# Half of the S5 chunk matrices made in the prologue, a third adaLN part made in the projections, products in stored order

## The chip, the cores and the metric

One core of one Trainium2 chip runs one inference step through two trunk layers. The metric is the device time of the whole program in microseconds (us).

## The reference, cut to what matters

```python
def trunk_layer(x, cmod, P, l, cache):
    sh1, sc1, g1, sh2, sc2, g2 = adaln(cmod, P['w_mod'][l], P['b_mod'][l])   # silu(c) @ w_mod + b, six parts
    h = rmsnorm(x, P['g_norm1'][l]) * (1.0 + sc1) + sh1
    z, xbc, dt_raw, u, dq, dk, dv, wq, wk, wv = split(h @ P['w_in'][l])
    # four mixers: SSD (z, xbc, dt), S5 (u), differential attention (dq, dk, dv), windowed attention (wq, wk, wv)
    merged = sum_i sigmoid(h @ w_gate + b_gate)_i * (y_i @ w_branch_i) @ P['w_out'][l]
    x = x + g1 * merged                                       # g1 is the third adaLN part
    h2 = rmsnorm(x, P['g_norm2'][l]) * (1.0 + sc2) + sh2
    return x + g2 * (square(relu(h2 @ P['w_fc1'][l])) @ P['w_fc2'][l])

def s5_direction(u, lam, log_step, b, c, s0):                 # per group of 16 channels, 64 complex states
    ab = exp(lam * exp(log_step)); coef = (ab - 1) / lam
    s[t] = ab * s[t-1] + coef * (b @ u[t]);  y[t] = real(c @ s[t])
```

There are 1024 channels, 640 tokens (128 of context, 512 latent), and everything is float32.

## The kernel before, in words

Activations lie with channels on partitions and 640 tokens along the free axis, in two halves of 320. A dense product is made from two-part operands: `load_w` loads a weight tile of 128x512, ACT rounds it to the high part `wh` (L211), and DVE or, for every third tile, POOL subtracts to get the low part `wl` (L195); each product is then three matmuls (L222 to L224). Weight loads are given priority ahead of the rest.

The order of the instructions on each engine is fixed when the program is built: a planner walks a simulated time line and issues what is ready, the earlier in the text first, so every engine runs a fixed queue in order. Within the "mix" stage the text itself is ordered by letter strings (`PLAN`, L58 to L72): each letter advances one generator (L1637 to L1660) by one step. In the string `pre`, which runs first, `b` is a step of `s5_build`, `u` of the S5 input projection, `v` of the keys and values of the windowed attention, `g` a gate panel, `d` a step of `adgen`, the adaLN parts made ahead.

The program starts with a prologue (L1550 to L1608). Its loop over q = 0..4 makes the adaLN parts 0 and 1 (shift and scale) in four panels (`panel_adaln`, L1562, and `adaln`, L278: matmuls of L287, a copy by ACT at L292, matmuls with `sel` at L294, the sum on DVE at L297), from 512 KB loads into a ring of 14 tiles `wm`; loads x; takes the norm (L352 to L371) and makes the normed activations `h` in high and low parts as panels come (`norm_mod`, L376 to L403, on DVE, ACT and POOL); and multiplies the first two tiles of the S5 input projection (L1593). After the loop it makes adaLN part 2 in four more panels (L1599).

`s5_build` (L473 to L672) turns the S5 parameters into chunk matrices. Its first step is a setup of some hundred operations on 128x32 tiles, mostly on DVE (L484 to L582). Then come eight builds, one for every four groups: `bt` and `bz` (L606 to L615); the input-side product `pt` (L625 to L628), made by `cmul`, which multiplies once on DVE into `s5u` (L592), once on POOL into `s5v` (L593) and combines on DVE (L594), twice for 128x512 elements; its transposes through PSUM (L633) and a copy (L636) to DRAM; the output-side product `qt` in the same way (L640 to L644); and the kernel matrix `pk` (L646 to L671). A build writes three times 512 KB to DRAM. Setup and builds are held back until the last element of `h` is made: POOL copies that element into a tile that they write next (L486, L608). One setup and eight builds thus run behind the prologue, the builds all in `pre`. Layer 1 has its own setup and eight builds inside the MLP of layer 0.

`pt` is stored in the order (group, channel m, position s) but computed in the order (group, s, m): its inner index m steps by 8 elements in the result (L626).

Of the kernel before, what the change touches and what calls it, by code (L numbers as in the profile page):

```python
# [13 lines left out]
F32 = mybir.dt.float32  # L14
# [4 lines left out]
ALU = mybir.AluOpType  # L19
# [34 lines left out]
SCAN = 5  # L54

LOW = 3
WM = 14
PLAN = dict(  # L58
    ad_out=((2, 2, 2, 1, 1), (0, 0, 0, 0, 0)),
    pre=("bbbuuvbubvbvbgvgggbvgvv", ""),  # L60
    mix=(
        "sisppppppiiippsisisasgssssappsssaxssgpsappxgxaaiagaaaagxcgaoogoccxcclooxscggcglgllccglPgogcgAPPA"
        "zPAAzcAAzwPzzzmmzPzPoozwPPwwwPwwAPwwmAmAmmnmmAPnnmnPnnninnfcqqcffwqkkqqfffkkkqkkkfkqkfwqhwwfhkfh"
# [12 lines left out]
def hybrid_body(ctx: ExitStack, tc: tile.TileContext, a: dict, o: dict, dbg: dict):  # L76
# [47 lines left out]
    def pb1():  # L124
        return pp.tile([128, 512], F32, tag="pb", name=nm("pb"), bufs=1)
# [11 lines left out]
    def ring(tag, cols, where="pool"):  # L137
        def get(shape, name, dt=F32):
            n = int(np.prod(shape[1:]))
            t = top[where].tile([128, cols], dt, tag=tag, name=nm(name), bufs=RINGS[tag])[:, :n]  # L140
            if len(shape) == 2:
                return t
            letters = "abcdef"[: len(shape) - 1]
            dims = dict(zip(letters, shape[1:]))
            return t.rearrange(f"p ({' '.join(letters)}) -> p {' '.join(letters)}", **dims)

        return get
# [3 lines left out]
    t1, tx, tq = ring("t1", 320), ring("tx", 652), ring("tq", 256)  # L151
    ty, tw, td = ring("ty", 1024, "right"), ring("tw", 648, "right"), ring("td", 640, "right")

    nt, wa = ring("nt", 320), ring("wa", 512)

    def big(shape, tag, dt=F32, bufs=1, where="pool"):

        return top[where].tile(list(shape), dt, tag=tag, name=nm(tag), bufs=bufs)
# [311 lines left out]

    s5m = {}

    def s5_build(l, where, after):  # L473

# [121 lines left out]
        for b in range(8):  # L598
            g0 = 4 * b
            late = after()  # L600
            braw = big([128, 2, 4, 16], "s5b", bufs=2, where=where)
            sp.dma_start(out=braw, in_=a["s5_b"][l, b])
            craw = big([128, 2, 4, 16], "s5c", bufs=2, where=where)
            sp.dma_start(out=craw, in_=a["s5_c"][l, b])

            bt = big([128, 2, 4, 16], "s5bt", where=where)  # L606
            if late is not None:
                nc.gpsimd.tensor_copy(out=bt[0:1, 0, 0, 0:1], in_=late)  # L608
            cmul(bt[:, 0], bc(cre, g0, 16), braw[:, 0], bc(cim, g0, 16), braw[:, 1], ALU.subtract, [128, 4, 16])
            cmul(bt[:, 1], bc(cre, g0, 16), braw[:, 1], bc(cim, g0, 16), braw[:, 0], ALU.add, [128, 4, 16])  # L610
            bz = big([128, 2, 4, 80], "s5bz", where=where)
            nc.gpsimd.memset(bz, 0.0)
            nc.vector.tensor_copy(out=bz[0:64, :, :, 0:16], in_=bt[0:64])
            nc.vector.tensor_copy(out=bz[64:128, :, :, 16:32], in_=bt[64:128])
            nc.vector.tensor_copy(out=bz[:, :, :, 48:64], in_=bt)  # L615

            shape = [128, 4, 8, 16]

            def ex(pt, ri):
                return pt[:, ri].rearrange("p s g -> p g s")[:, g0:g0 + 4].unsqueeze(3).to_broadcast(shape)  # L620

            def eb(mt, ri):
                return mt[:, ri].unsqueeze(2).to_broadcast(shape)

            pt = big([128, 2, 4, 16, 8], "s5pt", where=where)  # L625
            pv = pt.rearrange("p r g m s -> p r g s m")  # L626
            cmul(pv[:, 0], ex(pin, 0), eb(bt, 0), ex(pin, 1), eb(bt, 1), ALU.subtract, shape)
            cmul(pv[:, 1], ex(pin, 0), eb(bt, 1), ex(pin, 1), eb(bt, 0), ALU.add, shape)  # L628
            psb = big([128, 2, 512], "s5ps", where=where)
            for ri in range(2):  # L630
                ps = pb1()
                for g in range(4):
                    nc.tensor.transpose(  # L633
                        ps[:, g * 128:(g + 1) * 128], pt[:, ri, g].rearrange("p m s -> p (m s)"), ident
                    )
                nc.scalar.copy(out=psb[:, ri], in_=ps)  # L636
            nc.scalar.dma_start(out=pr_d[b], in_=psb)

            ncr = big([128, 2, 4, 16], "s5nc", where=where)
            nc.vector.tensor_scalar(out=ncr, in0=craw, scalar1=-1.0, scalar2=None, op0=ALU.mult)  # L640
            qt = big([128, 2, 4, 8, 16], "s5qt", where=where)
            cmul(qt[:, 0], ex(pou, 0), eb(craw, 0), ex(pou, 1), eb(craw, 1), ALU.subtract, shape)
            cmul(qt[:, 1], ex(pou, 1), eb(ncr, 0), ex(pou, 0), eb(craw, 1), ALU.subtract, shape)
            sp.dma_start(out=q_d[b], in_=qt.rearrange("p r g t m -> p r (g t m)"))  # L644

            pk = pb1()  # L646

            with tc.high_priority(offset=VISIT):
                for c0, c1, z0, t0 in ((0, 112, 16, 1), (128, 240, 0, 0)):
                    for ri in (1, 0):  # L650
                        for g in range(4):
                            nc.tensor.matmul(
                                pk[32 * g:32 * g + 32, c0:c1], bz[:, ri, g, z0:z0 + 32],
                                qt[:, ri, g, t0:t0 + 7].rearrange("p t m -> p (t m)"), start=(ri == 1), stop=(ri == 0),
                            )
                for ri, cc in ((0, craw[:, 0]), (1, ncr[:, 1])):
                    for g in range(4):
                        nc.tensor.matmul(
                            pk[32 * g:32 * g + 32, 112:128], bz[:, ri, g, 48:80], cc[:, g], start=(ri == 0),
                            stop=(ri == 1),  # L660
                        )
            ksb = big([128, 240], "s5ks", where=where)
            nc.scalar.copy(out=ksb, in_=pk[:, 0:240])
            nc.vector.scalar_tensor_tensor(
                out=ksb[:, 112:128], in0=i16, scalar=dtile[:, b:b + 1], in1=ksb[:, 112:128], op0=ALU.mult, op1=ALU.add
            )

            sp.dma_start(
                out=k_d[g0:g0 + 4].rearrange("g m s c -> (g m) s c"),
                in_=bass.AP(tensor=ksb.tensor, offset=ksb.offset, ap=[list(ksb.ap[0]), [16, 8], [1, 128]]),  # L670
            )  # L671
            yield  # L672

    i16 = load_const("i16", a["i16"], [128, 16], late)


    def s5_store(us):
# [867 lines left out]

    u_d = u_tiles(0)
    build = right("build0")
    build_after = [None]
    s5gen = s5_build(0, "build", lambda: build_after[0])
    with tc.tile_pool(name="pro", bufs=1, reuse_waits="tile") as pool:  # L1550
        top["pool"] = pool
        x = big([128, KT, T], "x")
        acc_n = big([128, T], "acc_n")
        h = h_tiles("h")

        accs, rb = mx(), mx()
        us = [big([128, 8, NI], "us0", bufs=2) for _ in range(2)]
        evs = [s5_store(u) for u in us]
        sums = [[dn(), dn()], [pb1(), None]]
# [11 lines left out]

        for q in range(5):
            if q < 4:
                panel_adaln((0, 1), q, accs[:, q % 2], rb[:, 0, HF + 8 * q:HF + 8 * q + 8])
                make_gsc(0, 0, 2 * q, 2)
            if q == 0:
                for k in range(KT):
                    sp.dma_start(out=x[:, k], in_=x_d[:, k])
                    for hf in range(2):
                        square_into(acc_n, x, k, hf)  # L1580
                for hf in range(2):
                    norm_spread(norm_factor(acc_n, hf)[0], rb, hf)
                sums[1][1] = pa()
                norms = [norm_mod(0, 0, x, rb, hf, *h) for hf in range(2)]
                continue
            for hf in range(2):
                step(norms[hf], 2)
            if q < 3:
                ws.append(load_ws(a["w_u"][0, q - 1], ahead=0))
            for k in {2: range(4), 3: range(4, 6), 4: range(6, 8)}.get(q, ()):  # L1590
                for w, ps in zip(ws, sums):
                    for hf in range(2):
                        mm3_step(ps[hf][:, :HF], split_w(w, k), hsl(h, k, hf), k == 0, k == KT - 1)  # L1593
        for ev, ps, u, d in zip(evs, sums, us, u_d):
            for hf in range(2):
                ev(hf, ps[hf][:, :HF])
            nc.scalar.dma_start(out=d, in_=u)
        accs = mx()
        for q in range(4):  # L1599
            panel_adaln((2,), q, accs[:, 0, (q % 2) * 256:], accs[:, 1, 8 * q:8 * q + 8])  # L1600
        load_all(late)
        maskf = t1([128, 2, 128], "mask")
        sp.dma_start(out=maskf, in_=a["wmask"])
        nc.vector.tensor_copy(out=maskb, in_=maskf)
        nc.vector.tensor_copy(out=identb, in_=ident)
        build_after[0] = h[1][0:1, KT - 1, T - 1:T].bitcast(F32)
        step(s5gen)
        adgen = adaln_ahead(0, range(3, 6), {4: 1})  # L1608

    for l in range(L):  # L1610
        acc_d = [dp.tile([128, T], F32, name=f"acc{l}_{f}") for f in range(KT)]
        with tc.tile_pool(name=f"mix{l}", bufs=1, reuse_waits="tile") as pool:
# [70 lines left out]
            def run(plan):  # L1683
                for what in plan:
                    advance(what)

            run(PLAN["pre"][l])
            if l == 0:
                build.__exit__(None, None, None)
            outer = right(f"outer{l}")  # L1690
            held = right(f"right{l}")
# [275 lines left out]
```

## Time and profile before

| | |
|---|---|
| times of three runs | 3071.25, 3073.83, 3077.72 us (median 3073.83) |
| profiled execution | 3075.0 us, of which the span from first to last instruction is 3073.2 us |
| PE (matmuls) busy | 2892.0 us, 94% of the span |
| DVE busy | 1759.4 us, 57% |
| ACT busy | 1175.9 us, 38% |
| POOL busy | 952.9 us, 31% |
| mean granted TensorE clock | 0.962 |

Busy time is that of an engine's instructions; overlapping matmuls are counted once. "Granted clock" is the share of full speed (2.4 GHz) that TensorE was given; it has two levels, 1.2 and 2.4 GHz, so a mean of 0.86 is a mix of both.

### The profile page before, as it was taken

The page shows a single profiled execution, that of the slowest core. Times are in us where ns is not written, and L with a number is a line of the kernel's source. Part 1 is how long each engine was busy: PE and PEld are TensorE (multiplying, and loading weights), DVE is VectorE, ACT ScalarE, POOL GpSimd, SP SyncE. Part 2 cuts the span into 40 slices and gives each one's busy share as a digit, 9 for nine tenths or more (in the row PEclk, how much of TensorE's full clock was granted, in tenths as well). Part 3 has the DMA queues.
Part 4 walks back from the last instruction along what each step waited for, and adds up shares of the span by engine and source line. Part 5 has one row for each costly group of instructions (what it writes and reads, how often), then busy time and mean ns, then how long its engine had stood idle before and what let it go on. Part 6 is the DMA issues. An engine that isn't in the chain of part 4 may idle for free. (4 is left out here: it accounts for less than half of the span.)

```text
span 3073.2 us, 54263 instructions
## 1 busy us (share of the span) xinstructions
PE 2892.0 (94%) x20782; PEld 2691.9 (88%) x20782; DVE 1759.4 (57%) x3866; ACT 1175.9 (38%) x2660; POOL 952.9 (31%) x1058
## 2 busy tenths in 40 slices
PE   8778898999899999999999889989999999999999
PEld 6768888788689989899999879978988899999999
DVE  5977936766553456656235786475666426533333
ACT  4234453244344342323234435423435433422323
POOL 1656503532221322334112670264131122211111
PEclk8888998899899999999999999989999999999999
DMA  8453253222532635445444323432243323222222
GB/s 284 156 183 108 75 142 99 83 76 91 171 117 68 221 122 172 142 131 163 146 149 142 112 80 109 135 102 61 90 151 100 100 87 123 62 76 76 76 76 83
DMA packets 240708, 364.23 MB, mean 119 GB/s; under 512 B 42144, under 2 KB 104352, under 8 KB 240448
## 3 DMA queue, kind: packets, MB, share of 16 engines
q1 hardware_dynamic: 225696, 336.97, 35.1%
q10 hardware_dynamic: 14752, 23.78, 2.1%
q8 instruction: 164, 2.69, 0.4%
q14 instruction: 96, 0.79, 0.1%
HBM read 294.98 MB, written 65.68 MB: 117 GB/s over the span
## 5 line engine op out<-in xcount | busy, mean ns | idle before, releaser
L195 POOL TENSOR_TENSOR wl<-wr,wh 128x512 fp32r<-128x512 f32 x207 | 279.5, 1350 | 1257.4 <-ACT wh L211 1215.1
L211 ACT CAST wh<-wr 128x512 fp32r<-128x512 f32 (+1 forms) x614 | 378.1, 620 | 600.2 <-PE dn L223 534.3
L195 DVE TENSOR_TENSOR wl<-wr,wh 128x512 fp32r<-128x512 f32 (+1 forms) x407 | 315.4, 778 | 319.8 <-ACT wh L211 306.3
L224 PE MATMUL dn<-hh,wl 128*128 128x320 f32 x1328 | 421.8, 318 | 12.1 <-DVE wl L195 12.1
L222 PE MATMUL dn<-hh,wh 128*128 128x320 f32 x1328 | 425.4, 321 | 5.5 <-ACT gah L1470 4.1
L223 PE MATMUL dn<-hl,wh 128*128 128x320 f32 x1328 | 424.9, 320 | 2.4 <-DVE hl L400 2.4
L222 PE MATMUL dn<-fh,wh 128*128 128x320 f32 x1008 | 313.2, 311 | 2.5 <-DVE x L1528 2.5
L222 PE MATMUL dn<-nh,wh 128*128 128x320 f32 x992 | 310.1, 313 | 2.8 <-DVE r L1734 2.8
L223 PE MATMUL dn<-nl,wh 128*128 128x320 f32 x992 | 309.0, 312 | 3.8 <-DVE nl L400 1.4
L224 PE MATMUL dn<-fh,wl 128*128 128x320 f32 x1008 | 312.6, 310 | 0.0
L223 PE MATMUL dn<-fl,wh 128*128 128x320 f32 x1008 | 312.1, 310 | 0.0
L224 PE MATMUL dn<-nh,wl 128*128 128x320 f32 x992 | 307.4, 310 | 0.0
L223 PE MATMUL dn<-wl,hh 128*128 128x256 f32 (+1 forms) x880 | 258.9, 295 | 20.2 <-DVE wl L195 17.4
L224 PEld LDWEIGHTS dn<-hh,wl 128*128 128x128 f32 x1328 | 257.3, 194 | 18.0 <-DVE wl L195 13.8
L222 PEld LDWEIGHTS dn<-hh,wh 128*128 128x128 f32 x1328 | 257.1, 194 | 11.8 <-ACT gah L1470 4.7
L222 PE MATMUL dn<-wh,hh 128*128 128x256 f32 (+1 forms) x880 | 260.2, 298 | 6.0 <-ACT hsq L1184 2.8
L223 PEld LDWEIGHTS dn<-hl,wh 128*128 128x128 f32 x1328 | 257.9, 194 | 8.4 <-DVE hl L400 3.5
L224 PE MATMUL dn<-wh,hl 128*128 128x256 f32 (+1 forms) x880 | 257.1, 293 | 0.0
L1528 DVE SCALAR_TENSOR_TENSOR x<-dn,mod,x 128x192 f32<-128x192 f32 (+2 forms) x240 | 97.9, 436 | 210.8 <-PE dn L224 202.9
L222 PE MATMUL dn<-B,wh 128*128 128x320 f32 x640 | 205.3, 322 | 11.5 <-ACT B L824 3.6
L223 PE MATMUL dn<-B,wh 128*128 128x320 f32 x640 | 200.7, 314 | 0.0
L224 PE MATMUL dn<-B,wl 128*128 128x320 f32 x640 | 200.3, 313 | 0.0
(404 smaller groups left out, 6816.7 us busy)
## 6 DMA issues: line engine op xcount, KB each, us to landing
wr<-in_w_fc_dram SPq DMA_DIRECT2D x256, 256.0 KB, 2.8
wa<-in_w_mod_dram SPq DMA_DIRECT2D x144, 256.0 KB, 4.5
wr<-in_w_gate_dram SPq DMA_DIRECT2D x128, 256.0 KB, 2.8
wr<-in_w_tok_dram SPq DMA_DIRECT2D x80, 256.0 KB, 3.1
wr<-in_w_branch_dram SPq DMA_DIRECT2D x64, 256.0 KB, 3.0
acc<-gth SPq DMA_DIRECT2D x48, 320.0 KB, 3.1
gold<-acc SPq DMA_DIRECT2D x48, 320.0 KB, 3.3
wm<-in_w_mod_dram SPq DMA_DIRECT2D x24, 512.0 KB, 9.0
```

The lines of the kernel that those rows point to most:

```text
L195: engine.tensor_tensor(out=out, in0=full, in1=hi, op=ALU.subtract)
L211: nc.scalar.copy(out=hi, in_=raw)
L222: nc.tensor.matmul(ps, sh, vh, start=first, stop=False)
L223: nc.tensor.matmul(ps, sh, vl, start=False, stop=False)
L224: nc.tensor.matmul(ps, sl, vh, start=False, stop=last)
L1528: nc.vector.scalar_tensor_tensor(out=xs, in0=ps[:, c0:c1], scalar=mods[l][:, part * 8 + f, s:s + 1], in1=xs, op0=ALU.mult, op1=ALU.add)
```

## The change

- The `s5_build` generator of layer 0 no longer waits for `h`, and its first five steps (setup and four builds) are taken in the prologue loop, one at the end of each round. The PSUM tile of these builds is the second bank of the tile `accs`; all four panels of parts 0 and 1 now share the first bank. The other four builds stay in `pre`, with PSUM from `pb1()` as before.
- adaLN part 2 leaves the prologue. It is made by `adgen` in four steps `d` of `pre`, with 256 KB loads into a ring of eight tiles in a pool of its own, `ada0`, that is closed at the end of `pre`.
- `pt` is computed in the order in which it is stored; now the powers `pin` are read with a step of 32 elements and `bt` with its inner index repeated. This holds for both layers.
- `WM` goes from 14 to 16, `i16` is loaded with the early constants, and `pre` gets a new order.

```diff
-WM = 14
+WM = 16
-    pre=("bbbuuvbubvbvbgvgggbvgvv", ""),
+    pre=("uubvbuvbvbdgvgdggdvgdvv", ""),
@@ s5_build
-            pv = pt.rearrange("p r g m s -> p r g s m")
-            cmul(pv[:, 0], ex(pin, 0), eb(bt, 0), ex(pin, 1), eb(bt, 1), ALU.subtract, shape)
-            cmul(pv[:, 1], ex(pin, 0), eb(bt, 1), ex(pin, 1), eb(bt, 0), ALU.add, shape)
+            shape = [128, 4, 16, 8]
+            def ei(ri):
+                return pin[:, ri].rearrange("p s g -> p g s")[:, g0:g0 + 4].unsqueeze(2).to_broadcast(shape)
+            def em(ri):
+                return bt[:, ri].unsqueeze(3).to_broadcast(shape)
+            cmul(pt[:, 0], ei(0), em(0), ei(1), em(1), ALU.subtract, shape)
+            cmul(pt[:, 1], ei(0), em(1), ei(1), em(0), ALU.add, shape)
-                ps = pb1()
+                ps = bank()
@@ prologue
-    s5gen = s5_build(0, "build", lambda: build_after[0])
+    s5gen = s5_build(0, "build", lambda: None, lambda: build_bank[0] if build_bank else pb1())
         accs, rb = mx(), mx()
+        build_bank.append(accs[:, 1])
-                panel_adaln((0, 1), q, accs[:, q % 2], rb[:, 0, HF + 8 * q:HF + 8 * q + 8])
+                panel_adaln((0, 1), q, accs[:, 0], rb[:, 0, HF + 8 * q:HF + 8 * q + 8])
...
+            step(s5gen)
-        accs = mx()
-        for q in range(4):
-            panel_adaln((2,), q, accs[:, 0, (q % 2) * 256:], accs[:, 1, 8 * q:8 * q + 8])
+        build_bank.clear()
-        build_after[0] = h[1][0:1, KT - 1, T - 1:T].bitcast(F32)
-        step(s5gen)
-        adgen = adaln_ahead(0, range(3, 6), {4: 1})
+        adgen = adaln_ahead(0, range(2, 6), {4: 1})
@@ mix
+            if l == 0:
+                ada = right("ada0")
             run(PLAN["pre"][l])
             if l == 0:
+                ada.__exit__(None, None, None)
```

## Rows read from the trace of the kernel before

**Rows 1.** Busy time by stage; PE, PEld, DVE, ACT, POOL, granted clock, DMA share, GB/s.
```profile
0.00:20.00 20.00, 6.86 (x56) 3.10 (x56) 7.64 (x29) 8.68 (x19) 0.91 (x7) 0.80 0.91 339
20.00:75.00 55.00, 53.56 (x407) 42.76 (x404) 36.58 (x143) 28.12 (x67) 10.03 (x16) 0.89 0.78 270
75.00:94.00 19.00, 12.92 (x87) 12.50 (x87) 16.78 (x81) 3.86 (x13) 4.74 (x7) 0.82 0.22 80
94.00:214.00 120.00, 89.95 (x917) 83.89 (x916) 115.18 (x208) 36.19 (x82) 86.22 (x89) 0.86 0.54 175
214.00:420.00 206.00, 187.04 (x1228) 175.22 (x1228) 148.87 (x295) 98.76 (x197) 97.85 (x159) 0.92 0.35 107
```

**Rows 2.** Waits of PE, 94 to 214: us in total, times, longest.
```profile
PE pa L1194 <- DVE wkn L1169: 5.2, 1, 5.2
PE pb L652 <- DVE s5bt L594: 5.1, 1, 5.1
PE dn L223 <- DVE wl L195: 3.9, 3, 2.9
...
PE dn L222 <- DVE dtraw L1206: 0.4, 1, 0.4
```

**Rows 3.** Timeline of PE: start, duration, instruction, [idle before, releaser].
```profile
83.73 0.59 PE L223 MATMUL dn<-wl,hh 128*128 128x272 f32 x1 [6.08 <-DVE wl L195]
```

**Rows 4.** Timeline of DVE: first and last step of the setup named below.
```profile
60.54 0.18 DVE L494 TENSOR_TENSOR s_zr<-s5prm,s_step 128x32 f32<-128x32 f32 x1
94.08 0.18 DVE L575 TENSOR_TENSOR s_cim<-s_t,s_rden 128x32 f32<-128x32 f32 x1
```

**Rows 5.** DVE busy at line L594 alone, 0 to 214.
```profile
0.00:214.00 214.00, 38.91 (x48) 0.86 0.61 206
```

**Rows 6.** DVE busy at line L592 alone, 0 to 214.
```profile
0.00:214.00 214.00, 34.09 (x48) 0.86 0.61 206
```

**Rows 7.** Groups by form, DVE, 94 to 214: xcount | busy us, mean ns | idle before.
```profile
L613 DVE COPY s5bz<-s5bt 64x128 f32<-64x128 f32 x8 | 3.8, 476 | 0.0
...
L615 DVE COPY s5bz<-s5bt 128x128 f32<-128x128 f32 x8 | 2.1, 268 | 0.1
```

**Rows 8.** Line L594, 0 to 214: duration ns min/median/max, first and last start.
```profile
L594 DVE TENSOR_TENSOR s5pt<-s5u,s5v x16: 1109/1192/2203, 98.7 to 202.0; 128x512 f32<-128x512 f32 x16
L594 DVE TENSOR_TENSOR s5qt<-s5u,s5v x16: 673/682/1284, 106.8 to 209.2; 128x512 f32<-128x512 f32 x16
```

**Rows 9.** Line L592, 0 to 214.
```profile
L592 DVE TENSOR_TENSOR s5u<-s5pin,s5bt x16: 678/686/1794, 95.1 to 196.7; 128x512 f32<-128x512 f32 x16
```

**Rows 10.** Line L593, 0 to 214.
```profile
L593 POOL TENSOR_TENSOR s5v<-s5pin,s5bt x16: 1104/1522/1634, 95.2 to 198.7; 128x512 f32<-128x512 f32 x16
```

**Rows 11.** Groups by form, PE, 94 to 214: products of the builds.
```profile
L633 PE MATMUL pb<-ident,s5pt 128*128 128x128 f32 x64 | 10.7, 293 | 4.4 <-DVE s5pt L594 3.7 <-ACT s5ps L636 0.7
...
L658 PE MATMUL pb<-s5nc,s5bz 128*32 128x16 f32 x64 | 2.1, 194 | 0.0
```

**Rows 12.** Waits of DVE, 0 to 214.
```profile
DVE mod L297 <- PE mx L294: 10.1, 4, 3.8
```

**Rows 13.** Timeline of POOL: the last low part of `h`.
```profile
55.31 0.87 POOL L195 TENSOR_TENSOR hl<-nh,hh 128x320 fp32r<-128x320 f32 x1
```

**Rows 14.** Timeline of PE: one panel of part 2, and panel 0's wait.
```profile
10.28 1.05 PE L294 MATMUL mx<-sel,mrow 128*128 128x2 f32 x8 [0.70 <-ACT mrow L292]
60.32 1.07 PE L287 MATMUL mx<-wm,cpad 128*32 128x256 f32 x16
64.65 0.50 PE L294 MATMUL mx<-sel,mrow 128*128 128x2 f32 x4
```

**Rows 15.** DMA issues, 94 to 214: xcount, KB each, us to landing.
```profile
s5k<-s5ks SPq DMA_DIRECT2D x8, 512.0 KB, 4.2
```

**Rows 16.** Groups by form, ACT, 0 to 1000.
```profile
L797 ACT COPY sn<-B 64x648 f32<-64x648 f32 x8 | 10.9, 1362 | 6.5 <-PE pb L804 6.5
L905 ACT ACTIVATE xp<-cv 128x646 f32<-128x646 f32 x6 | 4.4, 741 | 5.5 <-DVE cv L901 5.1 <-DVE wl L195 0.5
```

More of the change, by code (lines that the diff above doesn't have):

```diff
@@ L152, in hybrid_body, with wa @@
     ty, tw, td = ring("ty", 1024, "right"), ring("tw", 648, "right"), ring("td", 640, "right")
-    nt, wa = ring("nt", 320), ring("wa", 512)
+    nt = ring("nt", 320)
+    def wa(shape, name):
+        return ring("wa", 512, "ada" if "ada" in top else "pool")(shape, name)
     def big(shape, tag, dt=F32, bufs=1, where="pool"):
@@ L471, in hybrid_body, with s5_build @@
     s5m = {}
-    def s5_build(l, where, after):
+    def s5_build(l, where, after, bank=lambda: pb1()):
         pr_d = dp.tile([8, 128, 2, 512], F32, name=f"s5p{l}")
@@ L615, in s5_build @@
             nc.vector.tensor_copy(out=bz[:, :, :, 48:64], in_=bt)
[L617 to L623, printed above, removed]
+            shape = [128, 4, 16, 8]
[3 more added lines that the diff above has]
+                return bt[:, ri].unsqueeze(3).to_broadcast(shape)
             pt = big([128, 2, 4, 16, 8], "s5pt", where=where)
-            pv = pt.rearrange("p r g m s -> p r g s m")
-            cmul(pv[:, 0], ex(pin, 0), eb(bt, 0), ex(pin, 1), eb(bt, 1), ALU.subtract, shape)
-            cmul(pv[:, 1], ex(pin, 0), eb(bt, 1), ex(pin, 1), eb(bt, 0), ALU.add, shape)
+            cmul(pt[:, 0], ei(0), em(0), ei(1), em(1), ALU.subtract, shape)
+            cmul(pt[:, 1], ei(0), em(1), ei(1), em(0), ALU.add, shape)
             psb = big([128, 2, 512], "s5ps", where=where)
             for ri in range(2):
-                ps = pb1()
+                ps = bank()
                 for g in range(4):
@@ L637, in s5_build, with ex, eb @@
             nc.scalar.dma_start(out=pr_d[b], in_=psb)
+            shape = [128, 4, 8, 16]
+            def ex(pt, ri):
+                return pt[:, ri].rearrange("p s g -> p g s")[:, g0:g0 + 4].unsqueeze(3).to_broadcast(shape)
+            def eb(mt, ri):
+                return mt[:, ri].unsqueeze(2).to_broadcast(shape)
             ncr = big([128, 2, 4, 16], "s5nc", where=where)
@@ L644, in s5_build @@
             sp.dma_start(out=q_d[b], in_=qt.rearrange("p r g t m -> p r (g t m)"))
-            pk = pb1()
+            pk = bank()
             with tc.high_priority(offset=VISIT):
@@ L672, in s5_build @@
             yield
-    i16 = load_const("i16", a["i16"], [128, 16], late)
+    i16 = load_const("i16", a["i16"], [128, 16], soon)
     def s5_store(us):
@@ L1547, in hybrid_body @@
     build = right("build0")
-    build_after = [None]
-    s5gen = s5_build(0, "build", lambda: build_after[0])
+    build_bank = []
+    s5gen = s5_build(0, "build", lambda: None, lambda: build_bank[0] if build_bank else pb1())
     with tc.tile_pool(name="pro", bufs=1, reuse_waits="tile") as pool:
@@ L1593, in hybrid_body @@
                         mm3_step(ps[hf][:, :HF], split_w(w, k), hsl(h, k, hf), k == 0, k == KT - 1)
+            step(s5gen)
         for ev, ps, u, d in zip(evs, sums, us, u_d):
@@ L1685, in run @@
                     advance(what)
+            if l == 0:
+                ada = right("ada0")
             run(PLAN["pre"][l])
             if l == 0:
+                ada.__exit__(None, None, None)
+                del top["ada"]
                 build.__exit__(None, None, None)
```

## Prediction

> **What bounds the kernel now.** I read the busy time by stage first [rows 1]. Almost all of the change lies ahead of 214 us, where the last of layer 0's builds ends, so the reader should ask which engine is short in each stretch there. Up to 20 us PE is idle for 13.1 us: x and the first panel have to arrive, and nothing in the diff brings them earlier. From 20 to 75 us PE is busy 53.6 of 55 us, while DVE is busy 36.6 and POOL 10.0. From 75 to 94 us PE idles 6.1 us, and from 94 to 214 us it idles 30.0 us; in this last stretch DVE is busy 115.2 of 120 us. So TensorE sets the pace in the prologue, and DVE behind it.
>
> The waits of PE say the same. From 94 to 214 us there are 13 groups of them, 30.2 us together (the first three and the last stand in [rows 2]); all but two small ones, together 1.1 us, end on a product of DVE or POOL. They are not only the builds' own tiles (`s5bt`): weight parts `wl` and the keys `wkn` come late too, because they stand in DVE's queue behind the builds. The wait between 75 and 94 us is one of 6.08 us for a `wl` [rows 3], and at that time DVE is in the setup, whose steps run from 60.5 to 94.1 us [rows 4].
>
> Two more losses. The granted clock is 0.82 and 0.86 in those two stretches [rows 1], that is, TensorE was at 1.2 GHz in 36% and 28% of them; work done there at half speed is (1 - 0.82) x 12.9 + (1 - 0.86) x 90.0 = 14.9 us. It fell in stretches where PE had idled.
>
> **What one build costs.** On DVE, L594 and L592 take 38.9 + 34.1 = 73.0 us for eight builds, 9.1 each [rows 5, 6]; five groups of copies and small products (first and last in [rows 7]) take 15.3 us, 1.9 each. So 11.0 us of DVE a build, and eight of them with little else fill the 115 us. On PE the four groups are 24.9 us, 3.1 a build [rows 11].
>
> **The change part by part.**
>
> (a) Four builds leave 94 to 214 us. DVE is relieved there of 4 x 11.0 = 44 us. What is left is about 71 us of DVE for some 95 us of time, so DVE is no longer the engine that sets the pace, and PE is. Of the 30.0 us of idle I take 17 as gone; the ends are 0 (the same waits stay, each a point of order in DVE's fixed queue) and 30. Four builds stay in the stretch and with them some waits for `s5pt` and `s5qt`; that is why I stay well under the whole. PE's work is no gain: 4 x 3.1 = 12.4 us move to the prologue, and part 2's 4 x (1.07 + 0.50) = 6.3 us [rows 14] come the other way.
>
> (b) The setup leaves 60 to 94 us. The wait of 6.08 us for a `wl` stands in it [rows 3, 4]. I take 4 us as gone, between 0 and 6.
>
> (c) With fewer idle stretches the clock should fall less often. Of 14.9 us I take 5, between 0 and 15.
>
> (d) What the prologue pays. Setup and builds now compete with the norm. DVE's largest wait there is 10.1 us in four pieces for the adaLN panels [rows 12], and from 20 to 75 us it is idle for 18.4 us [rows 1]. Into this go the setup (some 100 steps of 0.18 us [rows 4], about 15 us with its waits on ACT; the part of it that already ran before 75 us is not counted again, about 8) and up to 44 us of builds. 7 + 44 us do not fit into 18 us, so at least half of this work runs on past 75 us, or delays the norm. The norm's last piece is made at 55.3 + 0.9 us on POOL [rows 13], and PE can do nothing more of the input projections without it, while behind it gates and projections need little of DVE. In the text the norm's steps of each round stand ahead of that round's build, so the planner prefers them; but a build's steps already in DVE's and POOL's queues block what comes behind them, and POOL's six pieces of `h` wait with it. I take 8 us of new idle on PE. The ends are 0 (gaps only; the builds' own products fill PE) and 33 (setup and three whole builds ahead of the norm's end: 15 + 31 us, less the 13 or so of DVE's idle time that lie ahead of 55 us).
>
> (e) Edits at nothing, with what hides them. All panels of parts 0 and 1 share one PSUM bank, so a panel's matmuls now wait for ACT's copy of the panel before; panel 0's own wait for such a copy is 0.70 us [rows 14], PE's next matmuls stand behind it, and the DMA pace hides it; uncovered, 3 x 0.7 = 2.1 us. The 24 MB that the prologue then moves (339 x 20 + 270 x 55 us = 21.6 MB now [rows 1], less 4.2 of part 2, plus 4 x 3 x 0.52 MB of builds [rows 15] and 0.5 of their inputs) make 323 GB/s over 75 us, below the 339 of the first 20; two more `wm` tiles and the early `i16` change no landing while the DMA engines are that busy. Dropping POOL's copies of the last `h` element frees POOL, which bounds nothing. The four `d` steps issue 16 loads of 256 KB on SP's queue in `pre`; for the case that they do not hide, see the third rival. Layer 1's builds lie where I read no wait of PE on them: zero. All later work is planned anew, and a planner's order can lose or win a few waits: I put +2 for it, between -6 and +8.
>
> (f) The stored order. The median of an L594 product into `pt`, whose inner step is 8 elements, is 1192 ns, and of one into `qt`, which is in order, 682 ns [rows 8]. With `pt` in order two instructions a build save 0.5 us each, 8 us over layer 0. Against it, the two reads of `pin` on DVE (686 ns now [rows 9]) and the two on POOL (1522 ns [rows 10]) get an inner step of 32 elements. No row shows DVE reading so. The nearest are on ACT: a strided read of 648 elements takes 1362 ns and an ordinary pass over 646 takes 741 [rows 16], so a read with a large step can cost as much as a write. Bounds: from -8 us (reads cost nothing) to +8 us on DVE with POOL longer too; I take zero for the sum, since the ACT row is the nearest.
>
> A rule of the Trainium skill speaks here ("SBUF — State Buffer", section "Door 1: The DMA port swizzle"): SBUF serves lines of 16 bytes, accesses that stay in a line run at full rate, and each access to a new line pays. The trace agrees on the write, 1192 against 682 ns. By this rule the new reads pay as the old write did, on two engines where it was one, and the edit gains nothing or loses; this is the second rival.
>
> **The sum.** -17 - 4 - 5 + 8 + 2 + 0 = -16 us. Against the profiled execution that is a span of 3073.2 - 16 = 3057.2 us and, with 1.8 us around it, 3059.0. The median of the runs shown is 1.2 us below the profiled execution (3073.83 against 3075.0), so 3057.8; I say 3058.
>
> **The rivals.**
>
> 1. More comes back: the planner finds room for the builds in gaps only, all idle time and the clock of 75 to 214 us return. -30 - 6 - 15 + 4 + 2 = -45, some 3029 us. For it: both DVE and PE have idle time in complementary stretches [rows 1]. Against it: fixed queues never fit so well.
>
> 2. The change does not do what it says of the products: reading with a step of 32 elements costs DVE more than the ordered write saves, and POOL, on whose `s5v` the product waits, gets longer: 0.5 us more for each of 16 DVE reads and as much on POOL, half of it on the path: some 8 us worse, 3066 us.
>
> 3. A wait takes the place of the one removed: in `pre` the adaLN loads through a ring of eight tiles hold back SP's queue. Weight loads stand behind them, then ACT's rounding and DVE's `wl`, for which PE waits. One such wait cost 6.08 us [rows 3]; three of them eat the gain: 3074 us, no change. For it: the four panels sit close together in `pre`. Against it: that stretch moves 175 GB/s [rows 1] and loses 6.3 MB of writes.
>
> 4. Slower: the builds hold up the norm. DVE and POOL work through builds ahead of the last pieces of `h`, and PE stands. It decides from the point where the delay passes 24 us (the gains 17 + 4 + 5 less the 2 of (e)), that is, with 24 + 13 = 37 us of setup and builds ahead of the norm's end; with setup and three builds the delay is 33 us, and the time 3074 + 9 = 3083 us. For it: before, the code held the builds back behind `h` with an explicit dependency, and DVE's steps stretch to double when POOL multiplies beside them (maximum 1794 against a minimum of 678 ns [rows 9]). Against it: the norm is earlier in the text and waits for panels anyway.
>
> **How the numbers follow.** The forecast (3046 to 3066 us) gets 0.46, the first rival 0.09, the second 0.13, the third 0.14, the fourth 0.18. A measurement of this kernel can tell about 0.2%, 6 us, from no change: faster is below 3068, slower above 3080. Forecast, first rival and most of the second are faster: 0.66. The third and the rest of the second are within 0.2%: 0.15. The fourth, and a little of the third, is slower: 0.19. The range is 3034 to 3084 us: it cuts off half of the first rival and the upper half of the fourth.
>
> **What would show it.** In the trace after: `s5prm` and L494 ahead of 30 us and four groups of L633 before 80 us; DVE's busy share between 20 and 75 us above 0.85, and PE's idle time there up by about 8 us; the last piece of `h` at 55 to 65 us (a later one is rival four); the last build before 200 us; the waits of PE on `wkn`, `wl` and `s5bt` in the stretch behind the prologue halved; L594 into `pt` at 0.7 us, and L592 from `pin` at 1.1 us if its reads pay. It is wrong if DVE is still full up to 210 us, or if the idle time turns up again as waits of PE behind 214 us.

## The result: slower by 0.7%, and the profile after

The changed kernel takes 3093.49 us (median of four runs, 3092.81 to 3099.52) against 3072.94 us of the kernel before: the ratio is 1.0066 with a 95% interval of 1.0047 to 1.0085. The forecast was 3058 us, in a range that ended at 3084. What happened is the fourth rival, and something more.

The profiled execution, 3099.5 us with a span of 3097.7, is the slowest of the four; its differences are to be read with some 6 us of play. The stages of the changed kernel, columns as in [rows 1]:

```profile
0.00:20.00 20.00, 7.54 (x52) 3.95 (x56) 8.34 (x33) 9.46 (x22) 0.91 (x7) 1.00 0.89 302
20.00:75.00 55.00, 25.99 (x188) 18.89 (x181) 50.29 (x199) 10.88 (x22) 19.13 (x19) 0.74 0.53 189
75.00:94.00 19.00, 12.57 (x124) 10.12 (x124) 18.74 (x41) 6.39 (x15) 11.20 (x9) 0.68 0.41 138
94.00:214.00 120.00, 110.53 (x1032) 104.13 (x1033) 79.74 (x157) 49.09 (x111) 61.11 (x67) 0.94 0.69 227
214.00:420.00 206.00, 176.01 (x1145) 163.17 (x1145) 159.81 (x318) 88.21 (x187) 104.17 (x168) 0.89 0.26 82
```

Against [rows 1], PE idles 27.6 us more from 20 to 75 us (29.0 against 1.4), 20.2 us less from 75 to 214 us (15.9 against 36.1), and 11.0 us more from 214 to 420 us. The sum of these stages and the first is +17.7 us. The first instruction of the residual of layer 0 is at 1037.5 us before and at 1055.0 us after, so a loss of 17.5 us is complete before it. Of the smaller part that comes later, 3.9 us lie in the MLP of layer 0 (shown further down).

```profile
L1528 DVE SCALAR_TENSOR_TENSOR x<-dn,mod,x x240: 316/409/553, 1037.5 to 3069.4; 128x192 f32<-128x192 f32 x43, 128x320 f32<-128x320 f32 x40, 128x128 f32<-128x128 f32 x37
```

```profile
L1538 DVE SCALAR_TENSOR_TENSOR x<-dn,mod,x x240: 339/409/553, 1055.0 to 3093.9; 128x192 f32<-128x192 f32 x43, 128x320 f32<-128x320 f32 x40, 128x128 f32<-128x128 f32 x37
```

Where PE stood in the prologue: its waits from 20 to 75 us (us in total, times, longest), and its own timeline.

```profile
PE mx L635 <- DVE s5pt L597: 17.9, 2, 16.7
PE mx L662 <- DVE s5bt L597: 1.9, 1, 1.9
```

```profile
57.57 1.12 PE L635 MATMUL mx<-ident,s5pt 128*128 128x128 f32 x4 [16.69 <-DVE s5pt L597]
...
65.22 2.92 PE L290 MATMUL mx<-wm,cpad 128*32 128x256 f32 x32 [0.47 <-ACT s5ks L673]
68.86 1.05 PE L297 MATMUL mx<-sel,mrow 128*128 128x2 f32 x8 [0.72 <-ACT mrow L295]
...
78.77 0.63 PE L225 MATMUL dn<-hh,wh 128*128 128x320 f32 x1 [8.36 <-ACT hh L402]
```

The transposes of build 0 (L635) are the next thing in PE's queue at 40.9 us and wait 16.7 us for `pt`. Behind them stand the matmuls of the third adaLN panel (L290). Their releaser is the point to see: `ACT s5ks L673`, the copy of the last PSUM result of build 0. The panel writes the first bank of the tile `accs` and this copy reads the second, so the panel needs nothing of it; but both are one tile. Behind that panel stands the third quarter of the norm, which waits for it on DVE:

```profile
51.20 0.19 DVE L578 TENSOR_TENSOR s_cim<-s_t,s_rden 128x32 f32<-128x32 f32 x1
...
77.43 0.21 DVE L300 TENSOR_TENSOR mod<-mx,bmod 128x4 f32<-128x4 f32 x2
...
107.56 0.54 DVE L403 SCALAR_TENSOR_TENSOR hl<-nh,mod,hh 128x320 fp32r<-128x320 f32 x1
```

The setup ends at 51.4 us (94.3 before [rows 4]); the modulation of the third panel is made at 77.4 us, and the last low part of `h` on DVE starts at 107.6 us instead of 53.7:

```profile
53.66 0.54 DVE L400 SCALAR_TENSOR_TENSOR hl<-nh,mod,hh 128x320 fp32r<-128x320 f32 x1
```

The products of layer 0's builds, durations in ns as minimum/median/maximum: `pt` is quicker, its two factors are slower than in [rows 8 to 10].

```profile
L595 DVE TENSOR_TENSOR s5u<-s5pin,s5bt x16: 1003/1086/2223, 52.2 to 169.4; 128x512 f32<-128x512 f32 x16
L596 POOL TENSOR_TENSOR s5v<-s5pin,s5bt x16: 1349/2021/2269, 52.4 to 170.7; 128x512 f32<-128x512 f32 x16
L597 DVE TENSOR_TENSOR s5pt<-s5u,s5v x16: 678/693/1827, 56.8 to 174.1; 128x512 f32<-128x512 f32 x16
```

### The profile page after: what moved, and what is told of

It is laid out like the page before. It is cut to its first block, busy times and chain, and to the rows that moved or that the text cites. A ratio compares the mean times of both kernels' runs of the same rounds, so it can differ in the third digit from the quotient of the medians.

```text
span 3097.7 us, 54213 instructions
## 1 busy us (share of the span) xinstructions
PE 2897.0 (94%) x20782; PEld 2695.7 (87%) x20782; DVE 1758.7 (57%) x3866; ACT 1178.4 (38%) x2660; POOL 960.1 (31%) x1049
## 4 chain that ended last, share of the span: by engine, by line
PE 74%; DVE 15%; DMA 4%; issue 3%; ACT 2%; POOL 2%; SPq 1%; DVEq 0%; ACTq 0%; POOLq 0%
PE dn L225 20%; PE dn L226 20%; PE dn L227 20%; PE mx L1417 3%; PE mx L290 1%; DVE wl L198 1%; DMA sseg<-acum 1%; PE mx L1287 1%; PE mx L1454 1%; DVE B L767 1%; PE pb L1331 1%; DVE s5u L595 1%; PE mx L1325 1%; PE mx L1449 1%; DVE sc L764 1%
```

## The experiments

All ratios below are to the kernel before, from fresh runs of it in the same session (medians of 3076.6 to 3077.5 us there), with 95% intervals.

**e1: the builds get a PSUM tile of their own.** The panels take one tile, the builds another, and the second input tile's sums move to the tile that the panels had.

```diff
-        accs, rb = mx(), mx()
-        build_bank.append(accs[:, 1])
-        sums = [[dn(), dn()], [pb1(), None]]
+        acc1, two, rb = pb1(), mx(), mx()
+        sums = [[dn(), dn()], [two[:, 0], two[:, 1]]]
-                panel_adaln((0, 1), q, accs[:, 0], ...
+                panel_adaln((0, 1), q, acc1, ...
-                sums[1][1] = pa()
+                build_bank.append(pa())
```

> As the changed kernel, but the builds of the prologue get a PSUM tile of their own (the panels' sums go to one tile, the builds' transposes and products to another, the second input tile's sums to a third), so that no panel has to wait for a build's copy. Theory A (the shared tile chains panels 2 and 3 behind builds 0 and 1): the third panel's matmuls start before 35 us instead of at 65 us, the last low part of h is made by 70 us, PE's idle time from 20 to 75 us falls from 29 to under 10 us, and the time to 3060 to 3072 us. Rival B (the builds stand ahead of the norm on DVE and POOL by their place in the text, whatever the bank): the panels come early, but the last part of h is still made after 85 us and the time stays at 3083 to 3095 us.

Measured: 0.9973 (0.9962 to 0.9984), 3068.2 us. Theory A holds, rival B falls. Stages and panels of e1:

```profile
20.00:75.00 55.00, 50.73 (x330) 41.60 (x330) 50.48 (x215) 26.22 (x57) 14.92 (x18) 0.97 0.64 218
75.00:94.00 19.00, 15.40 (x161) 12.77 (x160) 18.91 (x27) 5.56 (x16) 16.74 (x15) 0.91 0.87 296
94.00:214.00 120.00, 98.75 (x963) 92.94 (x962) 98.53 (x188) 40.20 (x92) 75.90 (x75) 0.88 0.63 202
214.00:420.00 206.00, 186.86 (x1204) 173.30 (x1204) 152.19 (x298) 93.30 (x197) 97.82 (x155) 0.92 0.29 90
```

```profile
30.67 3.64 PE L290 MATMUL pb<-wm,cpad 128*32 128x256 f32 x32
...
40.82 0.64 PE L290 MATMUL pb<-wm,cpad 128*32 128x256 f32 x8
```

```profile
56.80 0.55 DVE L403 SCALAR_TENSOR_TENSOR hl<-nh,mod,hh 128x320 fp32r<-128x320 f32 x1
...
70.02 1.10 DVE L595 TENSOR_TENSOR s5u<-s5pin,s5bt 128x512 f32<-128x512 f32 x1
```

The third panel starts at 30.7 us and the fourth at 40.8, the last low part of `h` on DVE at 56.8 us. DVE is as busy from 20 to 75 us as in the changed kernel (50.5 and 50.3 us), but in another order: the first product of a build from `pin` starts at 70.0 us, behind the norm. So with a tile of their own the builds no longer come ahead of the norm: none of their products runs before it is done. PE idles 4.3 us from 20 to 75 us, and from 75 to 214 us 24.9 us against 36.1 before. The 11 us of new idle time behind 214 us are gone too (19.1 us, as before).

**e4: the four builds behind the loop in the text**, in the PSUM bank of `pre`.

```diff
-            step(s5gen)          # at the end of each round q > 0
         build_bank.clear()
+        step(s5gen, 4)
```

> As the changed kernel, but the four builds stand behind the prologue's loop in the text (the setup stays in its first round), so the norm is ahead of them everywhere. Theory A: no panel waits for a build, the last low part of h is made by 65 us, PE idles under 10 us from 20 to 75 us, and DVE is still relieved afterwards: 3055 to 3068 us. Rival D (DVE's relief before the scan is given back in the mix stage, where PE then waits for the scan): idle time from 214 to 420 us stays at 30 us or more and the time is 3068 to 3080 us.

Measured: 0.9981 (0.9970 to 0.9991), 3070.6 us; the last low part of `h` at 58.1 us. It says the same as e1 by another way. The time is 2.6 us above the end of Theory A's range and inside Rival D's, but Rival D's mark did not show: PE idles 18.3 us from 214 to 420 us.

```profile
214.00:420.00 206.00, 187.70 (x1254) 175.26 (x1254) 151.00 (x296) 101.70 (x202) 97.00 (x156) 0.95 0.36 109
```

**e2: the builds held behind `h` again**, the rest of the change kept.

```diff
-    s5gen = s5_build(0, "build", lambda: None, ...
+    s5gen = s5_build(0, "build", lambda: build_after[0])
-            step(s5gen)                     # in the loop
+        build_after[0] = h[1][0:1, KT - 1, T - 1:T].bitcast(F32)
+        step(s5gen)                         # behind it
-    pre=("uubvbuvbvbdgvgdggdvgdvv", ""),
+    pre=("bbbuuvbubvbvbdgvgdggdbvgdvv", ""),
```

> As the changed kernel, but setup and all eight builds of layer 0 are held back behind h again and run in pre, as before; adaLN part 2 stays in pre, the stored order stays. Theory A (the prologue's builds are the whole loss): 3066 to 3078 us. Rival C (the adaLN loads in pre, through a ring of eight tiles on SP's queue, hold up weights): 3082 us or more, with PE's waits for weight parts in pre longer than before by 8 us or more.

Measured: 1.0033 (1.0020 to 1.0046), 3086.2 us. Theory A falls: without any build in the prologue about 10 us of loss were left. The time lies in rival C's range, but its mark is missing: PE's waits for weight parts `wl` from 94 to 420 us are 17.0 us, against 15.7 before. Either the moved adaLN part or the stored order had to cost; e3 and e9 tell which.

**e3: the stored order alone**, the kernel before with the diff's `ei`, `em` and the two new `cmul` lines.

> The kernel before with the stored order of the input-side products alone. If the strided reads cost about what the strided write did: L594 into pt 0.68 us, L592 from pin about 1.0 us, time within 6 us of the kernel before. If the reads cost more (POOL's products longer by 0.5 us and on the path): 3078 to 3085 us. If the order is a gain: 3060 to 3067 us.

Measured: 1.0078 (1.0061 to 1.0094), 3098.6 us, worse than any of the three expectations. This one edit, on which I had put zero, costs 21 us by itself (difference of the medians). Its products (layer 0):

```profile
L592 DVE TENSOR_TENSOR s5u<-s5pin,s5bt x16: 997/1076/2134, 95.4 to 204.2; 128x512 f32<-128x512 f32 x16
L593 POOL TENSOR_TENSOR s5v<-s5pin,s5bt x16: 1343/1814/2242, 95.5 to 207.7; 128x512 f32<-128x512 f32 x16
L594 DVE TENSOR_TENSOR s5pt<-s5u,s5v x16: 677/686/1860, 100.4 to 211.3; 128x512 f32<-128x512 f32 x16
```

**e9: the move of adaLN part 2 alone** (with the 16 `wm` tiles and the early `i16`): e2 with the products in their old order.

> The kernel before with the move of adaLN part 2 into pre alone (and the 16 wm tiles, the early i16): no build in the prologue, old order of the products. If the move costs nothing: within 6 us of the kernel before. If its loads hold up weights on SP's queue: 8 us or more above it. e2, which has the stored order on top, was at 1.0033 of the kernel before, so by the loss that strided reads showed this should be at 0.99 to 1.00.

Measured: 1.0004 (0.9987 to 1.0020), 3077.1 us. The move costs nothing within its interval, and the 9 us between e2 and this run are the stored order's. Rival C falls with it.

**e5: the changed kernel with the old order of the products** (the two `cmul` lines of before).

> The changed kernel with the input-side products in their old order (strided write, ordered reads). Theory A (the shared PSUM tile chains the panels behind the builds) says that the idle time of PE from 20 to 75 us stays near 29 us and the time at 3080 us or more. Theory S (the stored order is the loss, since the kernel before lost 21 us with it alone): about 3072 us.

Measured: 1.0047 (1.0030 to 1.0064), 3091.3 us. Theory A holds here too: the shared tile still stops PE, which idles 27.5 us from 20 to 75 us, most of it in one wait, and 30.5 us from 214 to 420 us. The profiled execution, 3079.3 us, is the fastest of its seven, 12 us below their median.

```profile
PE mx L636 <- DVE s5pt L597: 15.1, 1, 15.1
```

```profile
214.00:420.00 206.00, 175.50 (x1138) 162.36 (x1137) 160.72 (x319) 87.65 (x187) 103.84 (x168) 0.89 0.27 85
```

**e6: e1 with the old order of the products.**

> The builds' own PSUM tile as in e1, and the old order of the products. If the stored order costs by itself (POOL's product from pin at 1.9 instead of 1.5 us), this is faster than e1 (0.997 of the kernel before): 0.990 to 0.995 of the kernel before, some 3050 to 3062 us. If the 21 us of the stored order alone came from a new order of the fixed queues and not from the reads, this lies within 6 us of e1, on either side.

Measured: 0.9923 (0.9910 to 0.9936), 3053.4 us: 24 us faster than the kernel before and 15 us faster than e1.

```profile
214.00:420.00 206.00, 189.39 (x1216) 174.45 (x1215) 153.85 (x303) 97.47 (x201) 98.76 (x156) 0.93 0.31 96
```

**e7: the stored order with `pin` packed**, on the kernel before. The setup's two copies write `pin` in the order (group, position); then neither reads nor writes of `pt`'s products step.

```diff
-        pin = big([128, 2, 8, 32], "s5pin", where=where)
+        pin = big([128, 2, 32, 8], "s5pin", where=where)
+        piv = pin.rearrange("p r g s -> p r s g")     # the two copies write piv
-                return pin[:, ri].rearrange("p s g -> p g s")[:, g0:g0 + 4].unsqueeze(2)...
+                return pin[:, ri, g0:g0 + 4].unsqueeze(2)...
```

> The kernel before with the stored order, but the powers pin are laid out by the setup so that the products read them in order: no strided read and no strided write in a build. If the strided reads are the loss of e3: L592 from pin back to 0.69 us, POOL's product to 1.5 us, L594 into pt 0.69 us, and the time at or below the kernel before (0.995 to 1.000). If the loss of e3 is that of a new order of the queues: anywhere within 10 us on both sides, as likely above as below.

Measured: 0.9961 (0.9947 to 0.9975), 3065.3 us. The order of the product is the same as in e3; only where `pin` lies differs, and the time differs by 33 us.

```profile
L593 DVE TENSOR_TENSOR s5u<-s5pin,s5bt x16: 677/684/1795, 95.9 to 191.9; 128x512 f32<-128x512 f32 x16
L594 POOL TENSOR_TENSOR s5v<-s5pin,s5bt x16: 1063/1479/1595, 96.1 to 193.8; 128x512 f32<-128x512 f32 x16
```

**e8: both cures together**, e1's tiles and e7's packed `pin`.

> The builds' own PSUM tile as in e1, with the packed pin of e7. If strided reads cost: DVE and POOL are lightest here and it is the fastest of all, 0.988 to 0.994 of the kernel before. If not: within 6 us of e1.

Measured: 0.9920 (0.9904 to 0.9937), 3052.3 us: with e6, whose interval it shares, the fastest version.

```profile
L597 POOL TENSOR_TENSOR s5v<-s5pin,s5bt x16: 1063/1480/1577, 72.5 to 169.6; 128x512 f32<-128x512 f32 x16
```

**e10 and e11: which engine's strided read costs.** The part of `pin` with `ri` = 0 is read by DVE alone and the part with `ri` = 1 by POOL alone, so each can be laid out by itself, on e8.

```diff
+        pin = big([128, 2, 256], "s5pin", where=where)
+        packed = [pin[:, r].rearrange("p (g s) -> p s g", s=8) if r != STRIDED
+                  else pin[:, r].rearrange("p (s g) -> p s g", s=8) for r in range(2)]   # e10: 0, e11: 1
```

> e8 with the part of pin that DVE reads (L595) laid out with a step of 32 elements again, the part that POOL reads packed. If the strided read costs on DVE: near e1 (0.997 of the kernel before). If it costs on POOL: near e8 (0.992). DVE's read 1.0 us, POOL's product about 1.5 us.

> e8 with the part of pin that POOL reads (L596) strided and the part that DVE reads packed. If it costs on POOL: near e1 (0.997), with POOL's product at 1.9 us and DVE waiting for it; if on DVE: near e8 (0.992).

Measured: 0.9966 (0.9954 to 0.9977) with DVE's part strided, 0.9956 (0.9942 to 0.9970) with POOL's. Each alone costs about 11 to 14 us against e8, so neither expectation was right as an either-or. The products of e10, then of e11:

```profile
L597 DVE TENSOR_TENSOR s5u<-s5pin,s5bt x16: 999/1080/1855, 74.4 to 174.8; 128x512 f32<-128x512 f32 x16
L598 POOL TENSOR_TENSOR s5v<-s5pin,s5bt x16: 1064/1778/1937, 74.5 to 176.7; 128x512 f32<-128x512 f32 x16
```

```profile
L597 DVE TENSOR_TENSOR s5u<-s5pin,s5bt x16: 677/688/1871, 72.4 to 168.9; 128x512 f32<-128x512 f32 x16
L598 POOL TENSOR_TENSOR s5v<-s5pin,s5bt x16: 1343/1782/1899, 72.6 to 170.8; 128x512 f32<-128x512 f32 x16
```

In e10 POOL reads packed data, its minimum is 1064 ns as in e8, but its median is 1778 ns, 0.3 us above e8's: DVE's longer read beside it lengthens it. The timelines show how. The first pair of products in e8, e10, e11 and e1, in this order:

```profile
72.30 0.69 DVE L596 TENSOR_TENSOR s5u<-s5pin,s5bt 128x512 f32<-128x512 f32 x1
72.46 1.45 POOL L597 TENSOR_TENSOR s5v<-s5pin,s5bt 128x512 f32<-128x512 f32 x1 [0.26 <-DVE s5bt L598]
```

```profile
74.38 1.07 DVE L597 TENSOR_TENSOR s5u<-s5pin,s5bt 128x512 f32<-128x512 f32 x1
74.54 1.79 POOL L598 TENSOR_TENSOR s5v<-s5pin,s5bt 128x512 f32<-128x512 f32 x1 [0.26 <-DVE s5bt L599]
```

```profile
72.43 0.69 DVE L597 TENSOR_TENSOR s5u<-s5pin,s5bt 128x512 f32<-128x512 f32 x1
72.59 1.75 POOL L598 TENSOR_TENSOR s5v<-s5pin,s5bt 128x512 f32<-128x512 f32 x1 [0.26 <-DVE s5bt L599]
```

```profile
70.02 1.10 DVE L595 TENSOR_TENSOR s5u<-s5pin,s5bt 128x512 f32<-128x512 f32 x1
70.19 2.11 POOL L596 TENSOR_TENSOR s5v<-s5pin,s5bt 128x512 f32<-128x512 f32 x1 [0.26 <-DVE s5bt L597]
```

The products overlap in the records, yet the pair lasts almost as long as the two would one after the other. From the start of DVE's product to the end of POOL's, where POOL's starts within 0.3 us of DVE's, the medians in layer 0 are 1.61 us with packed reads (e8), 1.95 with DVE's part strided (e10), 1.92 with POOL's (e11) and 2.25 with both (e1). The two increments, 0.33 and 0.31 us, add up to the 0.63 of both. So POOL's record contains time in which it stands behind DVE's product, and either step lengthens the pair.

The MLP of layer 0, where the eight builds of layer 1 run, gives the direct part without the prologue's disturbance. Its relu instructions (minimum/median/maximum in ns, then first and last start in us) before and in the changed kernel, e1, e6 and e8, in this order:

```profile
L1733 ACT ACTIVATE r<-dn x64: 427/434/439, 1122.1 to 1584.7; 128x320 f32<-128x320 f32 x64
```

```profile
L1747 ACT ACTIVATE r<-dn x64: 424/434/442, 1138.7 to 1605.2; 128x320 f32<-128x320 f32 x64
```

```profile
L1746 ACT ACTIVATE r<-dn x64: 424/434/441, 1113.9 to 1580.9; 128x320 f32<-128x320 f32 x64
```

```profile
L1739 ACT ACTIVATE r<-dn x64: 427/434/441, 1102.7 to 1563.6; 128x320 f32<-128x320 f32 x64
```

```profile
L1747 ACT ACTIVATE r<-dn x64: 427/434/439, 1103.8 to 1562.3; 128x320 f32<-128x320 f32 x64
```

From first to last: 462.6 us before, 466.5 in the changed kernel, 467.0 in e1, 460.9 in e6, 458.5 in e8; the same instructions take 462.8 us in e10 and 463.6 in e11. All profiles fall into groups by the layout alone: 466.5 to 467.8 us with strided reads (the changed kernel, e1 to e4), 460.9 to 463.4 with the strided write (before, e5, e6, e9), 458.5 and 459.2 with packed reads (e8, e7). Strided reads stretch this stage by 4 to 6 us against the strided write and by some 8 us against packed reads, and each engine's part, against e8, is about half of that (4.3 and 5.1).

## Why the prediction was wrong, step by step

**(a) and (b), the relief behind the prologue: right in sign; that the size fits is partly luck.** Forecast -17 and -4; PE's idle time from 75 to 214 us fell by 20.2 us, and DVE's busy time from 94 to 214 us from 115 to 80 us. But the stall had pushed work of the prologue into this stretch: PE was busy only 26.0 us from 20 to 75 us, against 53.6 before. In e1, without the stall, the idle time from 75 to 214 us fell by 11.3 us, about half of the forecast.

**(c), the clock: right in size there, and nothing on the whole.** Worked out as in the forecast, work lost at 1.2 GHz from 75 to 214 us fell from 14.9 to 0.32 x 12.6 + 0.06 x 110.5 = 10.7 us, so -4 against -5. But from 214 to 420 us the granted clock fell from 0.92 to 0.89, which takes 0.11 x 176.0 - 0.08 x 187.0 = 4.4 us back, and from 0 to 75 us the gain is half a microsecond. With the clock given to two digits, nothing is left of this term.

**(d), the price of the prologue: this step failed.** I took 8 us of new idle on PE; it was 27.6. PE's idle time stayed under the bound of 33, but the end of the norm, for which that bound was worked out, came 54 us later (107.6 against 53.7 us). (In working out that bound I also counted 13 us of DVE's idle time ahead of 55 us; from 20 to 55 us the trace of before has 10.9.) The fourth rival named the place, but not what started it. I let builds block the norm through DVE's and POOL's queues and argued that "the planner prefers" the norm, whose steps stand ahead in the text. The block began in PE's queue and a PSUM tile: (e) had the shared tile in sight, priced the wait of a panel for the panel before, 0.7 us, and missed that a build's transposes, products and copies use the other half of the same tile, and stand between one panel and the next. DVE's queue, which I had named, came second: the third panel's last sums are done at 69.9 us (L297), but its modulation starts only at 77.4, behind products of builds 1 and 2, and PE idles 8.4 us for it. With separate tiles and no other edit (e1) the idle time from 20 to 75 us is 4.3 us, less than the 8 forecast, and the norm does go ahead of the builds, as I had argued. What is shown is that separate tiles (e1), or builds behind the loop (e4), undo the chain, and that the panel's recorded releaser is the build's copy; how the planner keeps its records of a tile was not looked into.

**(e), later work: wrong in size.** Forecast +2. PE's idle time from 214 to 420 us rose by 11.0 us. In e5, which shares the tile, it is 30.5 us, in e1 and e6, which do not, 19.1 and 16.6: it belongs to the late prologue, not to the change of order as such. Idle time behind 214 us was one of the two signs that I had named for being wrong. The move of adaLN part 2 is nothing, as taken (e9), so the third rival falls.

**(f), the stored order: this step failed too.** I took zero, from -8 to +8; the edit alone is +21 us (e3). The second rival had the sign, at +8 us, but not the size. The single durations were inside the bounds: DVE's read went from 686 to 1076 ns, the write from 1192 to 686 ns, which is even on DVE, and POOL's product from 1522 to 1814 ns. What failed is the step from durations to time: the sum sets DVE's reads against DVE's write and puts POOL's longer product at nothing, as if it ran beside. In the traces a pair of products lasts nearly as long as its two parts together, so both reads count: 2.25 us a pair (e1) against 1.66 in the old order (e6), 0.6 us more, while the ordered write saves 0.5. Over the 16 pairs of a layer that is a loss of 1 to 2 us; how it grows to the 7 us by which the builds of layer 0 end later was not followed. The start of the last step of the last build of layer 0 moved from 213.6 to 220.8 us in e3 and to 208.2 in e7. By the Trainium skill's rule on lines of 16 bytes ("SBUF — State Buffer", section "Door 1: The DMA port swizzle") the new reads had to pay; the trace now agrees, 677 ns packed and 997 at a step of 32 elements on DVE, 1063 and 1343 ns on POOL (minima of e7 and e3). The Trainium skill's page "GPSIMD Engine Reference" (section "7. Performance pitfalls for Q7 kernels") gives half as much again per element for reads with a step above 8 bytes in the Q7 kernels that it measured; the product here, one of whose two inputs steps, went up by 26%.

The two losses do not add, and the price of the stored order depends on what stands around it: 21 us on the kernel before (e3), 15 with separate tiles (e1 against e6), 9 with adaLN part 2 moved (e2 against e9), and in the changed kernel about 6 (against e5), where the intervals overlap. Where PE waits for the panels, some of what the builds lose may cost nothing; that was argued, not tested.

**Still open.** e3's one profile is 28.5 us longer than that of before, more than the 21 us of the medians. Of the 28.5, 7 us lie in the builds of layer 0, 4 between them and the residual, and 4 in layer 0's MLP; 9.2 lie in layer 1's mixers, where no build runs, and 3 behind them. In the profiles of the other kernels the stretch of layer 1's mixers differs from that of before by -3.7 to +6.5 us, so a new order of the fixed queues there and the play between executions were not told apart. Only the builds' and the MLP's part of the 21 us, some 11, is shown to come from the reads. And e6 and e8 do not differ by more than their intervals: that packed reads beat the old order rests on e7, which is faster than the kernel before, and on the MLP's 458.5 and 459.2 against 460.9 to 463.4 us.

## What to carry to other kernels

Two halves of one tile were one thing to the planner here: before filling a free half, list what is ordered through the other half, since a fixed queue turns a needless order into a stall. Price a rearranged operand on all the engines that read it, look in a trace whether a pair of products on DVE and POOL runs side by side or in turns before you set one against the other, and look for the layout in which neither side steps; here two setup copies did it. When an edit is "about zero" by durations, try it alone: here it was as large as the whole result.

## What the runs showed of the hardware

A DVE product of 128x512 floats whose one input steps by 32 elements takes 1.00 us at the least instead of 0.68, about what a result that steps by 8 costs (1.11 at the least [rows 8]). A POOL product with such an input takes 1.34 instead of 1.06 us. And POOL's product beside a DVE product that steps takes 1.78 us in the median though its own data are packed (1.48 beside one that does not; e10 and e8). Issued together, such a pair takes 1.61 us packed, 1.95 or 1.92 with one engine's input strided and 2.25 with both (medians of layer 0 in e8, e10, e11, e1), close to the sum of the two and not to the longer one.
